# The causal mask of the prompt's attention: a product added to the logits, or GpSimd's affine_select on keep factors and betas

## The chip, the cores and the metric

The kernel runs on one core of one Trainium2 chip. The metric is device time in microseconds (us) of one execution. The kernel before took 1763.74 us, the median of 3 runs (1763.74 to 1766.75).

## What is computed

One layer of a hybrid decoder, for a prompt of 1024 new tokens and for 8 x 8 sampled tokens with a paged cache. An input projection feeds three mixers (RWKV-7, a short convolution, stick-breaking attention with 8 heads of 64); an output projection, a squared-ReLU MLP of 4096 and a gated per-layer embedding follow, all with residuals. The change lies in the prompt's stick-breaking attention:

```python
z = einsum('bqhd,bkhd->bhqk', q_blk, kf) * scale + bias_f
mask = k_pos[None, :] < q_pos[:, None]
log_beta = where(mask, log_sigmoid(z), -inf)
log_keep = where(mask, log_sigmoid(-z), 0.0)
later = cumsum(log_keep, axis=3, reverse=True) - log_keep
wts = exp(log_beta + later)
out = einsum('bhqk,bkhd->bqhd', wts, vf)
```

So a key at or after the query's own position has beta 0 and keep factor 1, and a weight is beta times the product of the keep factors of all later keys.

## The kernel before, in words

All products run on TensorE in fp32 split into a high and a low part (three matmuls for one). ScalarE makes the high part (a cast), VectorE or GpSimd the low part (a subtraction); for the MLP's weights that is the function `split_piece` (lines 1036 to 1044): the cast is L1042, the subtraction L1043 (GpSimd by default), and each piece has ten buffers. Weights come from memory through two raw buffers (L1036), with SyncE issuing the DMAs.

The attention is a generator, `attention`, called twice: for the query blocks of the first 512 positions (line 1006, interleaved with `convolution`, 5 of its emission steps to 4 of the attention's) and for the second 512 (line 1434). It goes over units (head, block of 256 queries), head outermost, and over two query tiles of 128 in each. For query tile i, `weights` handles the first L = 128 (i + 1) keys, in chunks of 512:

- L880: GpSimd writes a 1.0 behind the last keep factor.
- L884 and L887: two matmuls put q k into a PSUM bank (high and low parts stacked to 128 rows; q's parts are swapped in the second).
- L886: in the last chunk alone, between them, a third matmul adds `later` through the identity to the last 128 columns. `later` is 0 below the diagonal and -1e30 from it on; it is made once per call (lines 843 to 847) with a memset and an affine_select on GpSimd and a cast on ScalarE.
- L888 and L889: ScalarE takes the sigmoid of z + bias (beta) and of -z - bias (keep) from PSUM into SBUF.
- L890: VectorE turns keep into the running product from the right (a scan).
- L892: beta is multiplied by the shifted keep, on VectorE, or in the second call on GpSimd for odd tiles.

`values` runs AHEAD = 2 units later: it transposes the weights (L910, TensorE), splits them (L60 on ScalarE, L61 on VectorE) and multiplies them by v (L920, L921); L923 and L925 add the halves and a DMA stores the result. keep has 2 buffers in the first call and 3 in the second, beta 6 in both.

Around the attention, the first half runs beside the sampled tokens' RWKV part and the convolution (products L169 to L171), the second half beside the output projection, the MLP's `up` and the MLP's `down` of the first 512 positions (products L1062 to L1064). An `up` product of one bank has 24 matmuls, a `down` product 6. VectorE takes them out of three PSUM banks (`acc`): L1418 for `down`, L1351 for `up`, L1341 for the output projection. Between the two attention calls lie the load and transposes of the residual (L1248, L1249) and the first half of the output projection.

The program's order is not the order of the text: the framework (`schedule_with_timeline_sim=True`) writes each engine's queue by priority and by its own estimate of when each instruction is ready. Each engine then works through its queue strictly in that order, so that an instruction that waits holds all that stand behind it.

Of the kernel before, what the change touches and what calls it, by code (L numbers as in the profile page):

```python
# [21 lines left out]
F32 = mybir.dt.float32  # L22
F32R = mybir.dt.float32r
I32 = mybir.dt.int32
AF = mybir.ActivationFunctionType
ALU = mybir.AluOpType
# [22 lines left out]
def hybrid_step(ctx: ExitStack, tc: tile.TileContext, I, O):  # L49
    nc = tc.nc  # L50
    V, S, G, PE, SP = nc.vector, nc.scalar, nc.gpsimd, nc.tensor, nc.sync
# [4 lines left out]
    def f(t):  # L56
        return t.bitcast(F32)

    def split(dst_hi, dst_lo, src):
        S.copy(dst_hi, src)  # L60
        V.tensor_sub(dst_lo, src, f(dst_hi))  # L61
# [60 lines left out]
    ident_r = consts.tile([128, 128], F32R)  # L122
# [105 lines left out]
    for s in range(2):  # L228
        hs = slice(64 * s, 64 * s + 64)
        for q in range(2):  # L230
            for kind in range(2):
                m = mfull[hs, q, kind, :]
                G.affine_select(m, m, pattern=[[1, 64]], compare_op=ALU.is_ge, fill=0.0, base=-kind,
                                channel_multiplier=-1)
                if q:
                    m3 = m.rearrange("p (g r) -> p g r", r=NJ)
                    G.affine_select(m3, m3, pattern=[[-NJ, 8], [0, NJ]], compare_op=ALU.is_ge, fill=0.0, base=0,
                                    channel_multiplier=1)
                    G.affine_select(m3, m3, pattern=[[NJ, 8], [0, NJ]], compare_op=ALU.is_ge, fill=0.0,
                                    base=NJ - 1, channel_multiplier=-1)  # L240
# [523 lines left out]
    ap = tc.alloc_tile_pool(name="att_a", bufs=1, side="right", reuse_waits="tile")  # L764
# [73 lines left out]

    def attention(ap, q0, q1, zbank, wbank, obank, AHEAD):


        neg = ap.tile([128, 128], F32, name="neg_f")
        G.memset(neg, 0.0)
        G.affine_select(neg, neg, pattern=[[-1, 128]], compare_op=ALU.is_ge, fill=-1.0e30, base=-1,
                        channel_multiplier=1)
        later = ap.tile([128, 128], F32R, name="later")
        S.copy(later, neg)
        bias = ap.tile([128, 2, 8], F32, name="bias")
        src = I["sb_bias"]
        SP.dma_start(bias[:, 0], bass.AP(tensor=src.tensor, offset=src.offset, ap=[[0, 128], [1, 8]]))  # L850
        V.tensor_scalar(bias[:, 1], bias[:, 0], -1.0, None, op0=ALU.mult)

        heads = {}

        def prep(h):

            stk = []
            for name, n, r0 in (("k", 1, 0), ("q", 0, 256 * q0), ("x", 0, 256 * q0)):
                r = slice(r0, 256 * q1)
                o = ap.tile([128, 256 * q1 - r0], F32R, name=f"stk_{name}", bufs=2)  # L860
                if name == "x":
                    for e in range(2):
                        SP.dma_start(f(o)[64 * e:64 * e + 64], stk_s[n, h, 1 - e, :, r])
                else:
                    SP.dma_start(f(o), stk_s[n, h, :, :, r].rearrange("e d t -> (e d) t"))
                stk.append(o)
            vs = ap.tile([128, 2 * q1, 128], F32R, name="vs", bufs=2)
            SP.dma_start(f(vs), v_s[h, 0:2 * q1].rearrange("i p e -> p i e"))
            heads[h] = stk + [vs]

        wts = {}

        def weights(h, qb):
            kk, qa, qx, _ = heads[h]
            for i in (2 * qb, 2 * qb + 1):
                L = 128 * (i + 1)
                q = slice(i * 128 - 256 * q0, i * 128 + 128 - 256 * q0)
                beta = ap.tile([128, 256 * q1], F32, name="beta", bufs=2 * AHEAD + 2)
                keep = ap.tile([128, 256 * q1 + 1], F32, name="keep", bufs=3 if q0 else 2)
                G.memset(keep[:, L:L + 1], 1.0)  # L880
                for c0 in range(0, L, 512):
                    n = min(512, L - c0)
                    pz = zbank()
                    PE.matmul(pz[:, :n], qa[:, q], kk[:, c0:c0 + n], start=True, stop=False)  # L884
                    if c0 + n == L:
                        PE.matmul(pz[:, n - 128:n], ident_r, later, start=False, stop=False)  # L886
                    PE.matmul(pz[:, :n], qx[:, q], kk[:, c0:c0 + n], start=False, stop=True)  # L887
                    S.activation(beta[:, c0:c0 + n], pz[:, :n], AF.Sigmoid, bias=bias[:, 0, h:h + 1])  # L888
                    S.activation(keep[:, c0:c0 + n], pz[:, :n], AF.Sigmoid, bias=bias[:, 1, h:h + 1], scale=-1.0)  # L889
                V.tensor_tensor_scan(keep[:, 0:L][:, ::-1], keep[:, 0:L][:, ::-1], onesq[:, 0:1].to_broadcast([128, L]),  # L890
                                     1.0, op0=ALU.mult, op1=ALU.mult)
                (G if i % 2 and q0 else V).tensor_mul(beta[:, 0:L], beta[:, 0:L], keep[:, 1:L + 1])  # L892
                wts[h, i] = beta

        def values(h, qb):
            vs = heads[h][3]
            pr, s = divmod(h, 2)
            d = slice(64 * s, 64 * s + 64)
            po = obank()
            last_kt = 2 * qb + 1  # L900
            for g in range(qb + 1):
                pw = wbank()
                wh = ap.tile([128, 2, 256], F32R, name="wth", bufs=2)
                wl = ap.tile([128, 2, 256], F32R, name="wtl", bufs=2)
                p3 = pw.rearrange("p (k q) -> p k q", k=2)
                for e in range(2):
                    kt = 2 * g + e
                    for i in range(2):
                        if 2 * qb + i >= kt:
                            PE.transpose(p3[:, e, i * 128:i * 128 + 128],  # L910
                                         wts[h, 2 * qb + i][:, kt * 128:kt * 128 + 128], ident)
                if g < qb:
                    split(wh, wl, p3)
                else:
                    split(wh[:, 0], wl[:, 0], p3[:, 0])
                    split(wh[:, 1, 128:], wl[:, 1, 128:], p3[:, 1, 128:])
                for e in range(2):
                    kt = 2 * g + e
                    c = slice(128 if kt == last_kt else 0, 256)
                    PE.matmul(po[:, c], vs[:, kt, :], wh[:, e, c], start=kt == 0, stop=False)  # L920
                    PE.matmul(po[:, c], vs[:, kt, :], wl[:, e, c], start=False, stop=kt == last_kt)  # L921
            tmp = ap.tile([128, 256], F32, name="tmp", bufs=2)
            S.copy(tmp[0:64], po[64:128, 0:256])  # L923
            o32 = ap.tile([128, 256], F32, name="o32", bufs=2)
            V.tensor_add(o32[d], po[0:64, 0:256], tmp[0:64])  # L925
            SP.dma_start(mix_s[4 + pr, d, qb * 256:qb * 256 + 256], o32[d])

        units = [(h, qb) for h in range(8) for qb in range(q0, q1)]
        prep(0)
        for n in range(len(units) + AHEAD):  # L930
            if n < len(units):
                if n % (q1 - q0) == 0 and units[n][0] < 7:
                    prep(units[n][0] + 1)
                weights(*units[n])
            if n >= AHEAD:
                values(*units[n - AHEAD])
            yield
# [66 lines left out]

    wkv_sample_chunk(banks(2))
    conv, att = convolution(), attention(ap, 0, 2, banks(3, 4), banks(5, 6), banks(7), AA)
    run(*[conv] * CA[0], *[att] * CA[1])
    cv.release()
# [423 lines left out]
    first = [page(pre, "kpg", krows, 0, n, 4) for n in range(PAGES)]  # L1432
    ap = tc.alloc_tile_pool(name="att_b", bufs=1, side="right", reuse_waits="tile")
    run(attention(ap, 2, 4, banks(3, 4), banks(5, 6), banks(7), AB_))
    ap.release()
    dp = tc.alloc_tile_pool(name="dec", bufs=1, side="right", reuse_waits="tile")
# [118 lines left out]
```

## Time and profile before

| what | us |
|---|---|
| median of 3 runs | 1763.74 |
| lowest, highest | 1763.74, 1766.75 |
| the profiled execution | 1762.9 |
| its span in the trace | 1761.2 |

| engine | busy us | share | instructions |
|---|---|---|---|
| TensorE, matmuls (PE) | 1686.2 | 96% | 11741 |
| TensorE, weight loads (PEld) | 1502.5 | 85% | 11741 |
| VectorE (DVE) | 1108.7 | 63% | 1826 |
| ScalarE (ACT) | 774.7 | 44% | 1539 |
| GpSimd (POOL) | 662.8 | 38% | 636 |

Times within the span are us from its start. A matmul's duration runs into the next one's, because matmuls are pipelined: what one takes from the engine is seen in the distance of the starts. An instruction's line is that of the program; an idle time before an instruction is written in brackets, with what ended it. Some matmul records are missing in a trace.

### The profile page before, as it was taken

The page shows a single profiled execution, that of the slowest core. Times are in us where ns is not written, and L with a number is a line of the kernel's source. Part 1 is how long each engine was busy: PE and PEld are TensorE (multiplying, and loading weights), DVE is VectorE, ACT ScalarE, POOL GpSimd, SP SyncE. Part 2 cuts the span into 40 slices and gives each one's busy share as a digit, 9 for nine tenths or more (in the row PEclk, how much of TensorE's full clock was granted, in tenths as well). Part 3 has the DMA queues.
Part 4 walks back from the last instruction along what each step waited for, and adds up shares of the span by engine and source line. Part 5 has one row for each costly group of instructions (what it writes and reads, how often), then busy time and mean ns, then how long its engine had stood idle before and what let it go on. Part 6 is the DMA issues. An engine that isn't in the chain of part 4 may idle for free.

```text
span 1761.2 us, 30286 instructions
## 1 busy us (share of the span) xinstructions
PE 1686.2 (96%) x11741; PEld 1502.5 (85%) x11741; DVE 1108.7 (63%) x1826; ACT 774.7 (44%) x1539; POOL 662.8 (38%) x636
## 2 busy tenths in 40 slices
PE   6999899999999899999999999998899999999998
PEld 5898888888888777888876666897899999998898
DVE  6266963554576669888763344447978787777432
ACT  6633323333343667666542433445534444435421
POOL 4123321212310453422344552446855555535210
PEclk9999998999999899999999999999999999999999
DMA  5134456433622753433244443521332323222211
GB/s 183 50 114 133 110 148 170 117 97 110 159 74 83 234 178 113 128 117 107 89 137 138 147 149 112 182 73 49 108 97 87 94 84 94 88 84 72 75 51 39
DMA packets 206737, 196.98 MB, mean 112 GB/s; under 512 B 57793, under 2 KB 172129, under 8 KB 206466
## 3 DMA queue, kind: packets, MB, share of 16 engines
q1 hardware_dynamic: 201474, 178.27, 34.1%
q0 software_dynamic: 5120, 16.78, 3.2%
q8 instruction: 92, 1.51, 0.4%
q14 instruction: 51, 0.42, 0.1%
HBM read 158.02 MB, written 36.98 MB: 111 GB/s over the span
## 4 chain that ended last, share of the span: by engine, by line
PE 73%; DVE 11%; DMA 4%; issue 4%; ACT 3%; POOL 2%; SPq 2%; ACTq 0%; DVEq 0%; POOLq 0%
PE b L1062 12%; PE b L1064 12%; PE b L1063 12%; PE b L1382 3%; PE b L1381 3%; PE b L1380 3%; PE b L169 2%; PE b L170 2%; PE b L171 2%; PE b L790 2%; PE b L791 2%; PE b L792 1%; PE b L910 1%; DVE base_Q L281 1%; PE b L1172 1%
## 5 line engine op out<-in xcount | busy, mean ns | idle before, releaser
L1043 POOL TENSOR_TENSOR wl<-wr,wh 128x512 fp32r<-128x512 f32 x172 | 239.1, 1399 | 317.7 <-ACT wh L1042 309.3
L1042 ACT CAST wh<-wr 128x512 fp32r<-128x512 f32 x292 | 179.2, 623 | 328.0 <-PE b L1063 227.5
L1418 DVE TENSOR_TENSOR x<-b,x 128x288 f32<-128x288 f32 (+1 forms) x384 | 199.1, 528 | 107.8 <-PE b L1064 100.1
L1062 PE MATMUL b<-ah,wh 128*128 128x288 f32 (+1 forms) x768 | 257.3, 335 | 8.6 <-DVE x L1418 5.8
L1064 PE MATMUL b<-ah,wl 128*128 128x288 f32 (+1 forms) x768 | 253.8, 331 | 0.0
L1063 PE MATMUL b<-al,wh 128*128 128x288 f32 (+1 forms) x768 | 252.8, 329 | 0.0
L1062 PEld LDWEIGHTS b<-ah,wh 128*128 128x128 f32 x768 | 145.5, 190 | 24.3 <-DVE x L1418 8.8
L1062 PE MATMUL b<-nh,wh 128*128 128x512 f32 (+1 forms) x448 | 164.5, 368 | 0.9 <-DVE x L1418 0.9
L1063 PE MATMUL b<-nl,wh 128*128 128x512 f32 (+1 forms) x448 | 165.1, 369 | 0.0
L1064 PE MATMUL b<-nh,wl 128*128 128x512 f32 (+1 forms) x448 | 164.0, 366 | 0.0
L1064 PEld LDWEIGHTS b<-ah,wl 128*128 128x128 f32 x768 | 145.4, 189 | 14.4 <-issue 4.1
L1063 PEld LDWEIGHTS b<-al,wh 128*128 128x128 f32 x768 | 145.6, 190 | 8.9
L790 PE MATMUL b<-wh,h_hi 128*128 128x256 f32 x432 | 130.6, 302 | 3.1 <-ACT nat L797 3.1
L792 PE MATMUL b<-wh,h_lo 128*128 128x256 f32 x432 | 128.0, 296 | 0.0
L791 PE MATMUL b<-wl,h_hi 128*128 128x256 f32 x432 | 127.9, 296 | 0.0
L169 PE MATMUL b<-h_hi,wh 128*128 128x384 f32 (+1 forms) x336 | 115.2, 343 | 1.9 <-ACT xs L330 1.2
L890 DVE TENSOR_TENSOR_SCAN keep<-keep,onesq 128x128 f32<-128x128 f32 (+3 forms) x64 | 93.4, 1464 | 36.0 <-ACT keep L889 35.1
L170 PE MATMUL b<-h_lo,wh 128*128 128x384 f32 (+1 forms) x336 | 113.3, 337 | 0.3 <-DVE h_lo L201 0.3
L171 PE MATMUL b<-h_hi,wl 128*128 128x384 f32 (+1 forms) x336 | 112.2, 334 | 0.0
L1043 DVE TENSOR_TENSOR wl<-wr,wh 128x512 fp32r<-128x512 f32 x120 | 101.1, 845 | 7.6 <-PE b L1064 3.9
L159 POOL TENSOR_TENSOR wl<-wr,wh 128x1024 fp32r<-128x1024 f32 x26 | 68.8, 2653 | 93.9 <-ACT wh L158 93.9
L1043 POOL TENSOR_TENSOR wsl<-s,wsh 128x512 fp32r<-128x512 f32 x64 | 88.6, 1406 | 28.3 <-ACT wsh L1042 28.2
(417 smaller groups left out, 4340.0 us busy)
## 6 DMA issues: line engine op xcount, KB each, us to landing
wr<-in_w_up SPq DMA_DIRECT2D x64, 512.0 KB
wr<-in_w_down SPq DMA_DIRECT2D x64, 512.0 KB
wr<-in_w_in SPq DMA_DIRECT2D x26, 512.0 KB
wr<-in_w_out SPq DMA_DIRECT2D x16, 512.0 KB
xt<-in_x_prompt SPq DMA_DIRECT2D x8, 512.0 KB
stk_s<-sth SPq DMA_DIRECT2D x32, 128.0 KB
stk_s<-stl SPq DMA_DIRECT2D x32, 128.0 KB
out<-nat SPq DMA_DIRECT2D x16, 256.0 KB
```

The lines of the kernel that those rows point to most:

```text
L169: PE.matmul(ps[:, :n], wh[:, k, c], a, start=(k == 0), stop=False)
L170: PE.matmul(ps[:, :n], wh[:, k, c], b, start=False, stop=False)
L171: PE.matmul(ps[:, :n], wl[:, k, c], a, start=False, stop=(k == nk - 1))
L790: PE.matmul(o, a, w[0][:, k, :], start=(k == 0), stop=False)
L791: PE.matmul(o, a, w[1][:, k, :], start=False, stop=False)
L792: PE.matmul(o, b, w[0][:, k, :], start=False, stop=(k == 7))
L1042: S.copy(h3, src)
L1043: (sub or G).tensor_sub(l3, src, f(h3))
L1062: PE.matmul(ps[:, :n], w(0, k, m), a, start=(k == 0), stop=False)
L1063: PE.matmul(ps[:, :n], w(0, k, m), b, start=False, stop=False)
L1064: PE.matmul(ps[:, :n], w(1, k, m), a, start=False, stop=(k == nk - 1))
L1418: V.tensor_add(p.x[:, m, t0:t0 + n], ps[:, :n], p.x[:, m, t0:t0 + n])
```

## The change

The mask leaves the logits. `neg_f`, `later` and the product L886 are gone. After both sigmoids of all chunks of a query tile, GpSimd overwrites the last 128 columns of keep with 1.0 and those of beta with 0.0 wherever the key is not before the query, in place, with one affine_select each.

```diff
@@ -838,13 +838,6 @@
     def attention(ap, q0, q1, zbank, wbank, obank, AHEAD):
-        neg = ap.tile([128, 128], F32, name="neg_f")
-        G.memset(neg, 0.0)
-        G.affine_select(neg, neg, pattern=[[-1, 128]], compare_op=ALU.is_ge, fill=-1.0e30, base=-1,
-                        channel_multiplier=1)
-        later = ap.tile([128, 128], F32R, name="later")
-        S.copy(later, neg)
         bias = ap.tile([128, 2, 8], F32, name="bias")
@@ -882,11 +875,14 @@
                     PE.matmul(pz[:, :n], qa[:, q], kk[:, c0:c0 + n], start=True, stop=False)
-                    if c0 + n == L:
-                        PE.matmul(pz[:, n - 128:n], ident_r, later, start=False, stop=False)
                     PE.matmul(pz[:, :n], qx[:, q], kk[:, c0:c0 + n], start=False, stop=True)
                     S.activation(beta[:, c0:c0 + n], pz[:, :n], AF.Sigmoid, bias=bias[:, 0, h:h + 1])
                     S.activation(keep[:, c0:c0 + n], pz[:, :n], AF.Sigmoid, bias=bias[:, 1, h:h + 1], scale=-1.0)
+
+                for t, fill in ((keep, 1.0), (beta, 0.0)):
+                    own = t[:, L - 128:L]
+                    G.affine_select(own, own, pattern=[[-1, 128]], compare_op=ALU.is_ge, fill=fill, base=-1,
+                                    channel_multiplier=1)
                 V.tensor_tensor_scan(keep[:, 0:L][:, ::-1], keep[:, 0:L][:, ::-1], onesq[:, 0:1].to_broadcast([128, L]),
                                      1.0, op0=ALU.mult, op1=ALU.mult)
```

## Rows read from the trace of the kernel before

**Rows 1.** The page, engines: busy us (share of the span) xinstructions.

```profile
PE 1686.2 (96%) x11741; PEld 1502.5 (85%) x11741; DVE 1108.7 (63%) x1826; ACT 774.7 (44%) x1539; POOL 662.8 (38%) x636
```

**Rows 2.** Windows by stage: length, busy us of each engine, clock, DMA.

```profile
core 0: us, PE busy (x) PEld busy (x) DVE busy (x) ACT busy (x) POOL busy (x), PEclk, DMA share, GB/s
...
572.00:597.00 25.00, 18.02 (x126) 15.88 (x125) 21.17 (x34) 20.31 (x46) 8.03 (x12) 0.81 0.91 283
...
633.00:673.00 40.00, 37.93 (x175) 31.04 (x176) 33.45 (x35) 28.43 (x53) 21.70 (x18) 0.96 0.50 157
673.00:867.00 194.00, 192.59 (x1035) 163.98 (x1033) 162.97 (x206) 128.37 (x254) 60.57 (x62) 1.00 0.37 113
```

**Rows 3.** Waits of TensorE, 572 to 597: us in total, times, longest.

```profile
PE b L920 <- DVE o L925: 2.8, 1, 2.8
```

**Rows 4.** Waits, 633 to 867, of TensorE's start, VectorE and ScalarE.

```profile
PE b L910 <- POOL beta L892: 1.4, 1, 1.4
PE b L884 <- DMA stk_q<-stk_s: 1.4, 1, 1.4
...
DVE keep L890 <- ACT keep L889: 17.4, 18, 1.7
...
ACT wh L1042 <- PE b L1063: 22.2, 24, 2.5
```

**Rows 5.** The mask product L886: durations, and its count by stage.

```profile
L886 PE MATMUL b<-later,ident_r x64: 219/223/328, 469.8 to 859.1; 128*128 128x128 f32 x64
...
447.00:572.00 125.00, 5.75 (x24) 4.54 (x24) 0.99 0.38 104
572.00:597.00 25.00, 2.05 (x8) 1.80 (x8) 0.81 0.91 283
```

**Rows 6.** TensorE's timeline from 794.8: start, us, line, operands.

```profile
794.80 0.40 PE L884 MATMUL b<-stk_k,stk_q 128*128 128x512 f32 x1
...
795.27 0.39 PE L884 MATMUL b<-stk_k,stk_q 128*128 128x512 f32 x1
795.50 0.22 PE L886 MATMUL b<-later,ident_r 128*128 128x128 f32 x1
795.56 0.44 PE L887 MATMUL b<-stk_k,stk_x 128*128 128x512 f32 x1
795.84 0.39 PE L1062 MATMUL b<-ah,wh 128*128 128x512 f32 x1
```

**Rows 7.** Groups of GpSimd by shape: busy us, mean ns, idle before.

```profile
L237 POOL TENSOR_SCALAR_AFFINE_SELECT mfull<-mfull 64x64 f32<-64x64 f32 x4 | 2.0, 534 | 0.1
...
L844 POOL TENSOR_SCALAR_AFFINE_SELECT neg_f<-neg_f 128x128 f32<-128x128 f32 x2 | 0.6, 323 | 0.1
```

**Rows 8.** Timeline, a weight piece handed from ScalarE to GpSimd.

```profile
767.55 0.63 ACT L1042 CAST wh<-wr 128x512 fp32r<-128x512 f32 x1
...
768.26 1.29 POOL L1043 TENSOR_TENSOR wl<-wr,wh 128x512 fp32r<-128x512 f32 x1 [1.97 <-ACT wh L1042]
```

**Rows 9.** Groups, 652 to 867: GpSimd's multiply into beta.

```profile
L892 POOL TENSOR_TENSOR beta<-beta,keep 128x768 f32<-128x768 f32 (+1 forms) x16 | 31.4, 1962 | 55.4 <-DVE keep L890 52.1 <-PE b L887 3.4
```

**Rows 10.** Timeline of VectorE, and GpSimd's split beside it, 559 to 593.

```profile
559.18 0.41 DVE L892 TENSOR_TENSOR beta<-beta,keep 128x256 f32<-128x256 f32 x1
...
575.39 0.42 DVE L890 TENSOR_TENSOR_SCAN keep<-keep,onesq 128x128 f32<-128x128 f32 x1 [1.85 <-ACT keep L889]
...
576.94 1.27 POOL L1043 TENSOR_TENSOR wl<-wr,wh 128x512 fp32r<-128x512 f32 x1 [0.52 <-ACT wh L1042]
...
577.04 1.45 DVE L892 TENSOR_TENSOR beta<-beta,keep 128x256 f32<-128x256 f32 x1
...
592.58 1.23 DVE L890 TENSOR_TENSOR_SCAN keep<-keep,onesq 128x512 f32<-128x512 f32 x1 [0.41 <-ACT keep L889]
```

**Rows 11.** Groups of VectorE by shape, 633 to 870: two scans.

```profile
L890 DVE TENSOR_TENSOR_SCAN keep<-keep,onesq 128x896 f32<-128x896 f32 x8 | 16.9, 2118 | 4.7 <-ACT keep L889 4.7
...
L890 DVE TENSOR_TENSOR_SCAN keep<-keep,onesq 128x640 f32<-128x640 f32 x8 | 11.9, 1490 | 5.9 <-ACT keep L889 5.4 <-POOL keep L880 0.5
```

## The prediction, made before the change was run

> **What bounds the kernel now.** I read the page first: TensorE is busy for 1686.2 of 1761.2 us [rows 1]. Then the windows by stage around the attention [rows 2]: the prompt's first half with the convolution as cover (447 to 572), a tail of eight query tiles after the convolution (572 to 597), and, past 633, the second half under the MLP's matmuls, with a ragged start and a dense rest. The reader is to see that TensorE stands for 25.00 - 18.02 = 7.0 us in the tail, while from 673 to 867 it is busy for 192.59 of 194.00 us, VectorE for 162.97 and GpSimd for only 60.57. So TensorE sets the pace, except in the tail; there the longest of its waits is one for VectorE's last addition of the attention, 2.8 us [rows 3]. At the second half's ragged start it waits twice, 1.4 us each, for the DMA of a query stack and for GpSimd's multiply into beta [rows 4].
>
> **What is removed.** 64 mask products, one per query tile: 24 before 572, 8 in the tail, 32 in the second half [rows 5]. Their durations (223 ns) overlap with those of their neighbours and are no price; I take starts instead [rows 6]. Two products of 512 columns without a mask take 795.27 - 794.80 = 0.47 us, the same two with the mask between them 795.84 - 795.27 = 0.57 us: 0.10 each there. In the tiles of 384, 256 and 128 columns the same subtraction gives 0.10 to 0.12. I take 0.11; bounds 0.06 (from the mask's start to the next product's, 795.50 to 795.56) and the 0.223 of its duration. Where TensorE is the bound all of it comes off: 24 + 32 = 56 products, 56 x 0.11 = **-6.2 us**. The eight of the tail I count at nothing, since TensorE waits there anyway. The two setups of the mask (memset, affine_select, cast) also go. I count them at nothing: at the second half's start, where the first product could wait for the mask, it waits for the DMA of its query stack [rows 4]; if the DMA came earlier, the 0.3 us of one affine_select could show. No DMA is added, removed or moved.
>
> **What is added.** Two affine_selects of 128x128 per query tile, 128 in all, on GpSimd. The same form took 323 ns on average; a 64x64 one with another pattern took 534, which is the upper bound [rows 7]. 128 x 0.32 = 41 us on an engine that is idle for 194 - 60.6 = 133 us of the dense stretch alone: as work it is free. What counts is where it stands. The scan (L890) followed ScalarE's keep sigmoid directly; now the keep affine_select stands between. Handing over to GpSimd costs 0.08 us (a cast ends at 767.55 + 0.63 = 768.18, the split begins at 768.26 [rows 8]), so each scan is ready 0.32 + 0.08 = **0.40 us later**. Bounds: nothing (the new order puts other VectorE work in front of the scan), and 0.53 + 0.08 + 1.96, when a multiply of GpSimd stands in front [rows 9]. I take 0.40, since GpSimd is mostly idle. The beta select follows 0.32 us later, under a scan of 0.42 us or more, and is hidden by it. If it weren't, the multiply, which in the second half runs on GpSimd itself for odd tiles, would be late by that 0.32.
>
> Where do 0.40 us count? In the dense stretch, nowhere: the weights of a tile are transposed two units (four tiles) after they are asked for, and VectorE already waits for the keep sigmoid 18 times, up to 1.7 us, without TensorE noticing [rows 4]. Behind a waiting affine_select on GpSimd stand the splits of the MLP's weights (L1043). They have ten buffers, and ScalarE, which feeds them, itself waits 24 times for TensorE to free one [rows 4]: a split may be late by microseconds. What would be late next, if that cover went, is the weight load of the next product.
>
> In the tail the cover is gone. Two of its eight scans find VectorE idle for the keep sigmoid (575.39 and 592.58), and the others share VectorE with work that is ready [rows 10]. I charge four tiles, between none and all eight: 4 x 0.40 = **+1.6 us**. At the start of the second half the 1.4 us wait for the multiply grows by one tile's 0.40: **+0.4 us** (bounds 0 and three tiles, 1.2).
>
> Sum: -6.2 + 1.6 + 0.4 = **-4.2 us**. The profiled execution took 1762.9 us (span 1761.2 and 1.7 around it), 0.84 less than the median of the runs, 1763.74. I take the difference off the median: **1759.5 us**. With the masks at 0.10 to 0.12 and the delays from none to 4.4 (eleven tiles), this case alone spans 1757.0 to 1762.5.
>
> **Sharing with VectorE.** A row speaks against the change: VectorE's multiply of 128x256 took 0.41 us at 559.18 and 1.45 at 577.04, when GpSimd ran a split from 576.94 [rows 10]. Two engines that read the same memory slow each other here, and in the tail VectorE has only 25.00 - 21.17 = 3.8 us to spare [rows 2]. No row shows whether a one-input affine_select does the same, so it is a rival, below.
>
> The Trainium skill, page "GPSIMD Engine Reference", section "1. Specifications", says that GpSimd's SBUF interfaces are shared with VectorE and contend with VectorE instructions that have two SBUF inputs. The scan and the multiply are such instructions; the trace agrees for the split (0.41 against 1.45 us). By that rule the sum would be +0.2 in place of -4.2.
>
> **The rivals.**
> (a) *VectorE slows beside each affine_select.* Each 0.32 us is added to VectorE. In the second half 64 x 0.32 = 20.5 us fit into its idle 40.00 - 33.45 + 194.00 - 162.97 = 37.6 us. In the tail 16 x 0.32 = 5.1 stand in place of 1.6, at the start of the second half 4 x 0.32 = 1.3 in place of 0.4: +4.4, so 1763.9. For it: the row just named (the page's rule is this case). Against: an affine_select reads one tensor, and few will overlap. Chance 0.09.
> (b) *The first half falls behind.* With two keep buffers its 24 covered tiles may each slip 0.40 us, 9.6 us in all, some two tiles at (572 - 470) / 24 = 4.25 us each, and these then stand without cover at 7.0 / 8 = 0.9 us: +1.8. All eight tail tiles are late as well, +1.6: 1762.9. Against it: the tiles come in bursts with pauses, so slips are made up. Chance 0.10.
> (c) *Slower: the scan queues behind GpSimd's multiply.* In the second half, a tile after an odd one may have its keep affine_select behind the odd tile's multiply (1.96 us, 16 times [rows 9]). Then the scan starts 1.96 + 0.40 = 2.4 us late and VectorE stands, with TensorE's PSUM evictions behind it. TensorE has three banks (`acc`); a down product fills one with 6 matmuls of 512 columns, 6 x 0.23 = 1.4 us (0.47 / 2 each), so VectorE may be away for 2.8 us. It decides when wait and scan together exceed that: 2.4 + 1.49 - 2.8 = 1.1 us eight times, 2.4 + 2.12 - 2.8 = 1.7 eight times [rows 11], 22 us; half of it, as the up products (24 matmuls to a bank) hide it: +11, 1770.5. For it: VectorE has little idle time. Against: GpSimd has 133 us free, and scans of 2 us pass without a stall today. Chance 0.18.
> (d) *The whole order is drawn anew.* The framework orders each engine's queue from its own estimate of the times, so 64 instructions less and 128 more can shift waits anywhere; before the attention and in the decoding, TensorE waits too. No part of the change sets the sign: 1754 to 1769. Chance 0.16, half of it faster, a third slower.
>
> **How the numbers follow.** The forecast has the remaining 0.47; its own span reaches over the bound of 0.2% (3.5 us, about what a measurement of this kernel can tell from no change, at 1760.2 and 1767.3), so 0.36 of it is faster and 0.11 the same. Faster: 0.36 + 0.08 = 0.44. Same: 0.11 + 0.09 + 0.10 + 0.03 = 0.33. Slower: 0.18 + 0.05 = 0.23. The range runs from just below (d)'s lower end to just past (c): 1753 to 1772.
>
> **What would show it.** Right: L884 and L887 follow each other within 0.47 us; the dense stretch is shorter by 32 x 0.11 = 3.5 us; affine_selects of 0.3 us with idle GpSimd time before them; the tail's TensorE idle time grows from 7.0 to about 8.6. Wrong: TensorE waits for evictions (L1418, L1351) in the second half, with scans waiting for GpSimd (c); multiplies that are stretched beside affine_selects (a); a tail of ten tiles (b); a shift in a stretch where no attention runs (d).

## The result, and the profile after

The changed kernel took 1752.03 us, the median of 5 runs (1744.33 to 1755.4), beside 1765.42 us of the kernel before in runs of the same kind (1763.74 to 1770.02). The ratio is 0.991, with a 95% interval of 0.9885 to 0.9935: faster by 0.9%. The two medians lie 13.4 us apart (0.8%), three times the 4.2 us forecast, and the time is 1 us below the range's lower end. The profiled execution took 1755.4 us, the longest of its five, so a comparison of the two traces shows less than the medians do: spans of 1753.7 and 1761.2 us, 7.5 us apart.

In the code after, L877 and L878 are the two products of a logit bank, L879 and L880 the sigmoids, L884 the affine_selects, L886 the scan, L888 the multiply, L906 the transposes, L916 and L917 the products with v, L921 the last addition, L1376 what is L1380 before. The page, engines, of the kernel after:

```profile
PE 1678.3 (96%) x11677; PEld 1494.9 (85%) x11677; DVE 1118.4 (64%) x1826; ACT 774.1 (44%) x1537; POOL 714.3 (41%) x760
```

Against [rows 1] TensorE has 64 instructions less and GpSimd 124 more (128 selects, less two memsets and two selects of the setups) and 51.5 us more of work. The sizes in time aren't to be read here. Windows put them in place. They are cut at six milestones that both traces have: the attention's first product, the convolution's last product (L171), the first product of the output projection, the first product of the attention's second half, its last product with v, and the last transpose of keys in the decode (the sampled tokens' attention). The first two bound what is called the first stage below, the second and third the tail. Before:

```profile
core 0: us, PE busy (x) PEld busy (x) DVE busy (x) ACT busy (x) POOL busy (x), PEclk, DMA share, GB/s
469.70:572.60 102.90, 99.52 (x796) 87.83 (x796) 69.01 (x126) 46.98 (x106) 8.00 (x28) 0.98 0.29 83
572.60:595.40 22.80, 15.82 (x118) 13.97 (x117) 19.57 (x31) 18.71 (x43) 6.71 (x12) 0.83 0.90 282
595.40:633.50 38.10, 36.17 (x170) 29.17 (x168) 15.49 (x31) 16.71 (x35) 24.21 (x25) 0.97 0.62 178
633.50:902.30 268.80, 265.48 (x1396) 225.15 (x1397) 216.06 (x274) 170.34 (x332) 91.31 (x84) 0.99 0.37 115
902.30:1067.30 165.00, 160.72 (x798) 112.70 (x797) 68.13 (x111) 60.80 (x114) 83.53 (x91) 0.98 0.52 156
```

The same five stages after:

```profile
469.05:564.50 95.45, 95.00 (x772) 83.83 (x772) 67.12 (x126) 47.28 (x106) 27.56 (x76) 1.00 0.30 85
564.50:589.10 24.60, 17.43 (x124) 14.57 (x123) 19.65 (x37) 20.86 (x49) 14.38 (x28) 0.82 0.91 301
589.10:620.70 31.60, 30.03 (x135) 24.32 (x134) 13.96 (x23) 12.05 (x25) 21.81 (x21) 0.93 0.69 193
620.70:899.10 278.40, 272.06 (x1396) 228.83 (x1397) 227.12 (x279) 172.82 (x338) 117.28 (x151) 0.99 0.38 111
899.10:1056.80 157.70, 154.92 (x789) 108.64 (x788) 68.58 (x110) 59.23 (x111) 83.17 (x90) 1.00 0.54 163
```

The convolution's stage is 7.45 us shorter, with 24 TensorE instructions less, and TensorE stands in it for 0.45 us (95.45 - 95.00) where it stood for 3.4; the clock there rises from 0.98 to 1.00. The second half is longer by 9.6 us and the stages on either side of it shorter by 6.5 and 7.3: 1396 instructions in both, of which 32 were mask products before, so MLP products have moved in from the neighbours. Stage by stage the last three can't be compared; from the output projection's first product to the first product of `up` for the second 512 positions (L1380, the same work in every kernel) it is 623.7 us before and 621.2 after.

**Where the first stage's time came from.** The timeline at its start, before (start, us, engine, line, operands, and in brackets the idle time and its end):

```profile
469.71 0.22 PE L884 MATMUL b<-stk_k,stk_q 128*128 128x128 f32 x1
469.77 0.27 PE L886 MATMUL b<-later,ident_r 128*128 128x128 f32 x1
471.63 0.32 PE L708 MATMUL b<-ident,s_in 64*64 64x64 f32 x2 [1.58 <-DMA s_in<-in_state_wkv]
471.88 0.33 PE L887 MATMUL b<-stk_k,stk_x 128*128 128x128 f32 x1
...
472.22 0.22 PE L886 MATMUL b<-later,ident_r 128*128 128x128 f32 x1
472.37 1.14 PE L708 MATMUL b<-ident,s_in 64*64 64x64 f32 x30
473.44 0.39 PE L887 MATMUL b<-stk_k,stk_x 128*128 128x256 f32 x1
...
477.11 1.15 PE L708 MATMUL b<-ident,s_in 64*64 64x64 f32 x32
...
479.08 0.69 ACT L888 ACTIVATE beta<-b,bias 128x512 f32<-128x512 f32 x1 [0.18 <-PE b L887]
...
482.14 2.36 POOL L159 TENSOR_TENSOR wl<-wr,wh 128x1024 fp32r<-128x1024 f32 x1 [3.87 <-ACT wh L158]
482.48 2.78 DVE L892 TENSOR_TENSOR beta<-beta,keep 128x512 f32<-128x512 f32 x2
...
485.11 0.74 PE L910 MATMUL b<-ident,beta 128*128 128x128 f32 x3 [1.80 <-DVE beta L892]
```

And after:

```profile
469.05 0.22 PE L877 MATMUL b<-stk_k,stk_q 128*128 128x128 f32 x1
469.11 0.27 PE L878 MATMUL b<-stk_k,stk_x 128*128 128x128 f32 x1
469.83 0.32 PE L708 MATMUL b<-ident,s_in 64*64 64x64 f32 x2 [0.45 <-DMA s_in<-in_state_wkv]
...
475.34 0.69 ACT L879 ACTIVATE beta<-b,bias 128x512 f32<-128x512 f32 x1 [1.02 <-PE b L878]
...
475.64 1.15 PE L708 MATMUL b<-ident,s_in 64*64 64x64 f32 x32
...
478.26 0.69 DVE L888 TENSOR_TENSOR beta<-beta,keep 128x512 f32<-128x512 f32 x1
...
479.24 2.55 POOL L159 TENSOR_TENSOR wl<-wr,wh 128x1024 fp32r<-128x1024 f32 x1
```

L708 transposes the sampled tokens' state, which comes by DMA. Before, it stood in TensorE's queue inside the groups of the first two tiles (a group is the products of one logit bank, from the first to the last), between the mask product and L887: the first group waited 1.58 us in its middle, the second ran 1.1 us of transposes before its last product. After, both groups are whole and L708 stands behind each. The fourth tile's group moved most: before, it stood behind a third run of L708 (477.11) and began 8.5 us into the stage (478.19); after, it stands ahead of that run (475.64) and began at 5.6 (474.68). Its beta sigmoid (512 columns) started 9.4 us after the stage's first product before (479.08), 6.3 after (475.34). So its multiply came at 482.48, beside GpSimd's split of a weight piece, and two of them took 2.78 us; after, it came at 478.26, ahead of that split, and took 0.69. TensorE's wait for it, 1.80 us, is gone, and with it a stretch at half the clock: windows of the granted clock (the column behind POOL), before

```profile
485.00:489.00 4.00, 3.90 (x15) 3.70 (x16) 4.00 (x6) 1.69 (x4) 2.56 (x3) 0.57 0.00 0
```

and after

```profile
485.00:489.00 4.00, 4.00 (x27) 3.87 (x26) 3.68 (x7) 2.38 (x5) 2.94 (x7) 1.00 0.56 174
```

TensorE is as busy in the one as in the other, but starts 15 instructions there in place of 27. Three terms make up most of the stage's 7.45 us: the 24 products less, 24 x 0.11 = 2.6; TensorE's waits, 3.38 - 0.45 = 2.9; and the slow stretch, where eight distances of 384-column products, 485.98 to 488.69, take 2.7 us and 8 x 0.17 = 1.4 would do, so 1.3. Together that is 6.8, an estimate.

### The profile page after: what moved, and what is told of

It is laid out like the page before. It is cut to its first block, busy times and chain, and to the rows that moved or that the text cites. A ratio compares the mean times of both kernels' runs of the same rounds, so it can differ in the third digit from the quotient of the medians.

```text
span 1753.7 us, 30271 instructions
## 1 busy us (share of the span) xinstructions
PE 1678.3 (96%) x11677; PEld 1494.9 (85%) x11677; DVE 1118.4 (64%) x1826; ACT 774.1 (44%) x1537; POOL 714.3 (41%) x760
## 4 chain that ended last, share of the span: by engine, by line
PE 73%; DVE 12%; DMA 5%; issue 5%; ACT 2%; POOL 2%; SPq 1%; ACTq 0%; POOLq 0%; DVEq 0%
PE b L1058 13%; PE b L1059 12%; PE b L1060 12%; PE b L1378 3%; PE b L1377 3%; PE b L1376 3%; PE b L169 2%; PE b L170 2%; PE b L171 2%; PE b L790 2%; PE b L791 2%; PE b L906 2%; PE b L792 1%; DVE base_Q L281 1%; DMA wr<-in_w_out 1%
## 5 line engine op out<-in xcount | busy, mean ns | idle before, releaser
L1039 POOL TENSOR_TENSOR wl<-wr,wh 128x512 fp32r<-128x512 f32 x172 | 247.0, 1445 | 298.7 <-ACT wh L1038 258.6
L1414 DVE TENSOR_TENSOR x<-b,x 128x288 f32<-128x288 f32 (+1 forms) x384 | 198.9, 527 | 103.0 <-PE b L1060 101.5
L171 PE MATMUL b<-h_hi,wl 128*128 128x384 f32 (+1 forms) x336 | 112.2, 334 | 0.0
L886 DVE TENSOR_TENSOR_SCAN keep<-keep,onesq 128x128 f32<-128x128 f32 (+3 forms) x64 | 94.7, 1481 | 24.5 <-POOL keep L884 24.3
```

The costliest lines, as they stand in the source:

```text
L171: PE.matmul(ps[:, :n], wl[:, k, c], a, start=False, stop=(k == nk - 1))
L1039: (sub or G).tensor_sub(l3, src, f(h3))
L1414: V.tensor_add(p.x[:, m, t0:t0 + n], ps[:, :n], p.x[:, m, t0:t0 + n])
```

## Experiments

All were timed in five rounds beside the kernel before, in three groups. Theory, at the start (A in the expectations): the removed products, where TensorE sets the pace, are the gain. Rival (B): the queues' new order is. C, put after the first four runs, names the part of the order: the place of the first groups in TensorE's queue.

**after_again.** The changed kernel a second time, no edit.

> The changed kernel once more, beside the others. If the measured gain (13 us by the medians, 7.5 between the two profiled executions) is a property of the program, its median lies 11 to 15 us under the kernel before here too. If the difference between 7.5 and 13 is scatter from execution to execution, the two medians lie 7 to 15 us apart, and the spread of either is several us.

1751.78 us (6 runs), ratio 0.992 (0.9892 to 0.9949). The gain repeats. Its stages are those of the first trace within 0.2 us up to the output projection (95.3 and 24.5); from there to L1380 it took 618.7, so 2.5 us of that long stretch is one execution's difference from another.

**no_mask.** Neither products nor selects; the causal mask is left out.

```diff
-                    if c0 + n == L:
-                        PE.matmul(pz[:, n - 128:n], ident_r, later, start=False, stop=False)
...
```

The set-up of the mask goes too.

> The mask is left out altogether (the output is that of an attention without the causal mask): no product, no affine_select. Theory A, prices: 64 products x 0.11 us = 7 us come off, and nothing waits for GpSimd, so it is 7 us faster than before and 0 to 2 us faster than the changed kernel would be by prices alone. Theory B, the order: what was gained beyond 6 us comes from the newly drawn order of the queues, so this third order may land anywhere from 2 to 20 us under the kernel before, and the waits in the convolution's stage differ from both.

1753.37 us (7 runs), ratio 0.9936 (0.9911 to 0.9961): no faster than the kernel that has 128 selects more. The first stage is 95.5 us, as after; the tail, with no select in it, is 25.6, the longest of all kernels.

**both_masks.** The products stay, and the selects come in.

```diff
                     S.activation(keep[:, c0:c0 + n], pz[:, :n], AF.Sigmoid, bias=bias[:, 1, h:h + 1], scale=-1.0)
+                for t, fill in ((keep, 1.0), (beta, 0.0)):
+                    own = t[:, L - 128:L]
+                    G.affine_select(own, own, pattern=[[-1, 128]], compare_op=ALU.is_ge, fill=fill, base=-1,
+                                    channel_multiplier=1)
```

> The product stays and the two affine_selects per tile are added. Theory A, prices: the affine_selects cost 2 us (four tail tiles and one start tile at 0.40), so 0 to 4 us slower than before. Theory B, the order: another draw, 5 us or more from the kernel before in either direction; faster than before by 3 us or more would show that the gain does not come from the removed product.

1755.34 us (12 runs), ratio 0.9952 (0.9933 to 0.9971). Work was only added, and the kernel is 8 to 9 us faster than before. Its first stage is 103.0 us, with the first two groups cut; its tail is 21.0 and its decode 156.5 in place of 165.0. No sum of the prices above can come out so.

**mask_last.** The same 64 products, each third in its group in place of second.

```diff
-                    if c0 + n == L:
-                        PE.matmul(pz[:, n - 128:n], ident_r, later, start=False, stop=False)
-                    PE.matmul(pz[:, :n], qx[:, q], kk[:, c0:c0 + n], start=False, stop=True)
+                    PE.matmul(pz[:, :n], qx[:, q], kk[:, c0:c0 + n], start=False, stop=c0 + n < L)
+                    if c0 + n == L:
+                        PE.matmul(pz[:, n - 128:n], ident_r, later, start=False, stop=True)
```

> The same work as before, with the mask product as the third of its group in place of the second. Theory A, prices: no difference, within 1.5 us. Theory B, the order: the framework draws a new order, and the time moves by 3 us or more either way though no work has changed.

1765.55 us (12 runs), ratio 0.9997 (0.9977 to 1.0017): no change. L708 stands again inside the first group (it waited 1.79 us there), now ahead of the mask product, and the first stage is 102.7 us. Theory A had no difference here, and so it came. If B holds, not every edit of this place redraws the order to advantage.

**head0_only and all_but_head0.** The change for 4 of the 64 tiles (head 0 of the first half), and for the other 60.

```diff
-                    if c0 + n == L:
+                    if c0 + n == L and not (not q0 and h == 0):
...
+                for t, fill in ((keep, 1.0), (beta, 0.0)) if not q0 and h == 0 else ():
```

all_but_head0 has the two conditions the other way round; the set-up of the mask stays in both.

> The change for 4 of 64 tiles alone: head 0 of the first half (its 4 tiles get affine_selects, all others keep the product). Theory A, prices: 4 x 0.11 = 0.4 us, within 1 us of before. Theory C, the place: in the queue of TensorE the first group of products (L884, L886, L887) is cut by a transpose of the sampled tokens' state (L708) that waits for a DMA; without the third product the group is whole and in front of it. Then the stage from the attention's first product to the convolution's last falls from 102.9 us to 97.5 to 99, the 2.0 us wait for the multiply at 482.9 and the half-clock stretch behind it are gone, and the kernel is 3 to 6 us faster.

> The change for 60 of 64 tiles: all but head 0 of the first half. Theory A, prices: 60/64 of the gain, so 10 to 12 us faster than before, the convolution's stage at about 96 us. Theory C, the place: that stage keeps the cut group, the 2.0 us wait and the half-clock stretch, and is only 20 x 0.11 = 2.2 us shorter, 100.5 to 101.5; the kernel is 5 to 9 us faster, with what the second half gives.

Four tiles: 1751.09 us (6 runs), ratio 0.9917 (0.9887 to 0.9948). Sixty tiles: 1764.18 (12 runs), 0.9989 (0.9965 to 1.0013). Four tiles bring the whole gain, the other sixty, with 60 products less, nothing that can be measured. Both theories missed these times: C had the four at 3 to 6 us faster, where 14 came, and the sixty at 5 to 9, where 1 came; A had 0.4 and 10 to 12. C's first stage came for the four tiles (97.5 to 99 expected) and for the sixty within 0.2 us. First stages: 98.1 and 101.7 us; the 20 other products of that stage are worth 1.2 to 2.6 us (102.9 - 101.7; 98.1 - 95.5), near 20 x 0.11 = 2.2, the place of the first groups 4.8.

**first_half and second_half.** The change in one call of the attention alone.

```diff
-                    if c0 + n == L:
+                    if c0 + n == L and q0:
...
+                for t, fill in ((keep, 1.0), (beta, 0.0)) if q0 == 0 else ():
```

second_half has the two conditions the other way round.

> The change in the first half's call alone. Theory C: the convolution's stage at 95.3 to 95.6 us as in the changed kernel, 7.4 us gained there; from the output projection's first product on as before (623 to 626 us), with the wait of over 4 us for a page of keys in the decoding and the half-clock stretch behind it. In all 6 to 9 us faster. Theory A, prices: 32 x 0.11 less what the tail costs: 1 to 3 us faster.

> The change in the second half's call alone. Theory C: the convolution's stage stays at 102.7 to 103.0; the second half gains its 32 x 0.11 = 3.5 us and the decoding's wait for a page of keys falls to 2.4 us or less with no half-clock stretch behind it, another 2 to 5 us: 4 to 8 us faster. Theory A, prices: 3 to 4 us faster, and the wait for the page as before, over 4 us.

1762.25 us (0.9983, 0.9965 to 1.0002) and 1767.33 us (1.0021, 0.9999 to 1.0043), 12 runs each. In first_half the groups are whole and the first stage is 96.1 us, but from the output projection to L1380 it takes 630.0: the 6 us are given back. In second_half the 32 products that the forecast priced at 3.5 us are gone, and that stretch takes 624.6, 0.9 more than before, and the wait for a page of keys is still 4.1. Neither time can be told from that of the kernel before, and C, which had them at 6 to 9 and 4 to 8 us faster, missed both. A came near with 1 to 3 us for first_half and missed second_half (3 to 4). The parts don't add up to the whole (-3 and +2 against -13), so the prices of the parts weren't the cause.

**What the decode shows.** The sampled tokens' attention takes its cached keys page by page, each by a DMA. TensorE's transposes of a page of keys, and what ended its idle time before them (us, times); kernel before:

```profile
L1167 PE MATMUL b<-ident,kpg x128: 270/273/473, 902.5 to 1067.4; 128*128 128x128 f32 x128
its engine sat idle before it (us, times) until:
  DMA kpg<-in_cache_k,idx: 4.1, 1
```

It is 4.1 to 4.4 us in before, mask_last, no_mask, all_but_head0, first_half and second_half, but 2.7 after (2.0 in after_again), 1.8 in both_masks and 0.5 in head0_only. It costs more than itself: timeline of before behind it,

```profile
926.62 1.11 PE L1167 MATMUL b<-ident,kpg 128*128 128x128 f32 x4 [4.12 <-DMA kpg<-in_cache_k,idx]
927.39 0.77 PE L1062 MATMUL b<-ah,wh 128*128 128x512 f32 x1
...
931.80 0.63 PE L1063 MATMUL b<-al,wh 128*128 128x512 f32 x1
932.23 0.52 PE L1064 MATMUL b<-ah,wl 128*128 128x512 f32 x1
...
935.14 0.40 PE L1063 MATMUL b<-al,wh 128*128 128x512 f32 x1
935.37 0.39 PE L1064 MATMUL b<-ah,wl 128*128 128x512 f32 x1
```

Products of 512 columns start 0.43 us apart at 932 and 0.23 at 935. From 927.39 to 932.23 there are 11 distances, 4.84 us where 11 x 0.23 = 2.5 would do: 2.3 us on top of the 4.1.

So the theory is now that the place of 4 tiles' products in TensorE's queue is the whole cause. The direct trial keeps all work and changes the place alone.

**whole_group and all_but_head0_whole.** The framework is asked to put the second and third product of head 0's groups in the first half straight behind the first; in the kernel before, and in all_but_head0.

```diff
                     PE.matmul(pz[:, :n], qa[:, q], kk[:, c0:c0 + n], start=True, stop=False)
-                    if c0 + n == L:
-                        PE.matmul(pz[:, n - 128:n], ident_r, later, start=False, stop=False)
-                    PE.matmul(pz[:, :n], qx[:, q], kk[:, c0:c0 + n], start=False, stop=True)
+                    with (tc.high_priority() if not q0 and h == 0 else ExitStack()):
+                        if c0 + n == L:
+                            PE.matmul(pz[:, n - 128:n], ident_r, later, start=False, stop=False)
+                        PE.matmul(pz[:, :n], qx[:, q], kk[:, c0:c0 + n], start=False, stop=True)
```

> All 64 mask products stay and no affine_select is added; the only edit asks the framework to place the second and third product of head 0's tiles in the first half (16 products' neighbours at most) straight behind the first one, so that no transpose of L708 stands inside a group. Theory 'place': in the queue of TensorE this kernel has head 0's groups where the changed kernel has them, and from there to the decode the order that the kernel with 4 changed tiles has. The stage from the first product of the attention's first half to the last of the convolution takes 97.5 to 99 us (102.9 before, 98.1 with the 4 tiles changed), the stretch at half clock inside it is gone, TensorE's wait for a page of keys in the decode is under 1.5 us (4.2 to 4.5 before), and the time is 1750 to 1753 us, though nothing of the mask's work has gone. Theory 'work' (rival: the removed products and the affine_selects' own times make the gain): the time is that of the kernel before, within 2 us, 1763 to 1767.

> 60 of the 64 tiles changed, head 0 of the first half keeps its 4 mask products, and the products of these 4 groups are placed one behind the other. Without the placing this kernel took 1764.2 us. Theory 'place': its queue is now that of the changed kernel with 4 products added, so it takes 1751 to 1755 us, the convolution stage 95.5 to 97. Theory 'work': placing 4 groups is worth at most the 4 products' 0.5 us, 1763 to 1765.

whole_group: 1753.64 us (8 runs), ratio 0.9927 (0.99 to 0.9955). No instruction of the mask has gone or come, and the gain is there, 0.7% beside 0.9% with intervals that overlap; the time is 0.6 us above the range that theory "place" gave. all_but_head0_whole: 1749.40 us (6 runs), 0.9911 (0.988 to 0.9941), 15 us faster than all_but_head0, which has the same instructions, and 1.6 us below its expected range. Theory "place" holds, "work" falls. whole_group's page, engines, has the instructions of [rows 1], one for one:

```profile
PE 1683.0 (96%) x11741; PEld 1501.6 (86%) x11741; DVE 1104.1 (63%) x1826; ACT 776.6 (44%) x1539; POOL 668.9 (38%) x636
```

Its timeline at the attention's start (L884, L887 and L888 are the three products):

```profile
469.96 0.22 PE L884 MATMUL b<-stk_k,stk_q 128*128 128x128 f32 x1
470.02 0.27 PE L887 MATMUL b<-later,ident_r 128*128 128x128 f32 x1
470.13 0.27 PE L888 MATMUL b<-stk_k,stk_x 128*128 128x128 f32 x1
471.04 0.33 PE L708 MATMUL b<-ident,s_in 64*64 64x64 f32 x2 [0.64 <-DMA s_in<-in_state_wkv]
```

its clock in the window where the kernel before had the half-clock stretch (0.96 there, as in mask_last),

```profile
480.00:520.00 40.00, 40.00 (x329) 37.50 (x330) 27.14 (x53) 18.52 (x47) 5.73 (x12) 1.00 0.17 55
```

and its wait for pages of keys:

```profile
L1168 PE MATMUL b<-ident,kpg x128: 270/273/331, 891.7 to 1050.2; 128*128 128x128 f32 x128
its engine sat idle before it (us, times) until:
  DMA kpg<-in_cache_k,idx: 0.2, 1
```

The first stage takes 98.5 us, as with the 4 tiles changed (98.1). No line of the edit touches the decode, 420 us later, yet the wait there falls from 4.1 to 0.2 us: the products of the MLP stand in other places between the pages. Counted in the traces, the products with weights between the decode's first five runs of page transposes are 19, 11, 27 and 12 before, and the same in mask_last; they are 20, 17, 23 and 16 in whole_group, and the same in head0_only. In all_but_head0_whole the first stage took 97.5 us where 95.5 to 97 were expected; its longest wait of TensorE there is another one, 1.3 us for a keep sigmoid.

**twice.** The changed kernel with every select issued a second time.

```diff
-                for t, fill in ((keep, 1.0), (beta, 0.0)):
+                for t, fill in ((keep, 1.0), (beta, 0.0), (keep, 1.0), (beta, 0.0)):
```

> The changed kernel with both affine_selects issued a second time on every tile (the result is the same): 128 more of 0.29 us on GpSimd. Theory 'added work is dear': each of the 64 tiles' scans starts some 0.6 us later, and where TensorE waits for it (4 tiles of the tail, the start of the second half) that is 2.4 to 3.0 us, 1754 to 1756. Theory 'the order decides': the longer path is hidden but for the tail's 2.4, and what the queue's new order does to the decode's pages is worth more than that either way: its order around the pages is that of the kernel with 4 changed tiles, so the wait for a page is under 1.5 us and the time 1750 to 1755.

1753.75 us (10 runs), ratio 0.9939 (0.9917 to 0.9962). By time the two theories can't be told apart. By stage they can: the tail, where a longer path of each tile should have shown, is 23.2 us, shorter than with single selects (24.6), and no transpose of keys waits for a page's DMA.

**pages5_after.** The changed kernel with a fifth buffer for pages of keys.

```diff
-                    kpg = first.pop(0) if first else page(pre, "kpg", krows, b, n, 4)
+                    kpg = first.pop(0) if first else page(pre, "kpg", krows, b, n, 5)
```

> The changed kernel with five buffers for pages of keys in the decode instead of four (it fits since the two tiles of the mask are gone). If TensorE's wait for a page in the decode (2.3 us there, 1.4 in the second profile) comes from a buffer that is late, it is gone and the time is 1749 to 1751; if it comes from the page's gather itself, issued when the decode's first pages are, a fifth page is on its way earlier and the queue's order is drawn anew: the time is within 3 us of 1752 on either side, and the wait stands at the sixth page instead of the fifth.

1750.61 us (7 runs), ratio 0.9917 (0.9884 to 0.9951). The wait for pages is gone altogether, and the time lies in both of the ranges expected; the interval lies over that of the change itself: a microsecond or two can't be told here. That the buffer alone did it isn't shown, since the order is another one too.

The kernels side by side, in us; "cut" says whether L708 stands inside a product group of the first two tiles, the first stage runs to the convolution's last product, the tail to the output projection's first:

| kernel | groups | first stage | tail | output projection to L1380 | wait for pages | median |
|---|---|---|---|---|---|---|
| before | cut | 102.9 | 22.8 | 623.7 | 4.1 | 1763.7 to 1765.4 |
| mask_last | cut | 102.7 | 22.7 | 625.5 | 4.4 | 1765.6 |
| all_but_head0 | cut | 101.7 | 25.1 | 622.2 | 4.4 | 1764.2 |
| second_half | cut | 102.4 | 23.0 | 624.6 | 4.1 | 1767.3 |
| both_masks | cut | 103.0 | 21.0 | 620.7 | 1.8 | 1755.3 |
| first_half | whole | 96.1 | 23.8 | 630.0 | 4.3 | 1762.3 |
| no_mask | whole | 95.5 | 25.6 | 617.1 | 4.3 | 1753.4 |
| after | whole | 95.5 | 24.6 | 621.2 | 2.7 | 1752.0 |
| twice | whole | 93.3 | 23.2 | 623.7 | 0 | 1753.8 |
| head0_only | whole | 98.1 | 23.1 | 617.3 | 0.5 | 1751.1 |
| whole_group | whole | 98.5 | 20.8 | 617.7 | 0.2 | 1753.6 |
| all_but_head0_whole | whole | 97.5 | 23.0 | 615.2 | 1.9 | 1749.4 |
| pages5_after | whole | 95.1 | 24.4 | 616.9 | 0 | 1750.6 |

The four kernels with cut groups and a long wait take 1764 to 1767 us, the six with whole groups and a wait of at most 2.7 take 1749 to 1754, the three that have one of the two lie at 1753 to 1762. Several are level with the change and none is measurably faster.

What "cut" stands for is more than the wait for the DMA. In all five kernels with cut groups the fourth tile's group stands behind the third run of L708 and begins 7.3 to 8.7 us into the first stage, and TensorE waits 1.8 to 2.3 us for VectorE about 15 us into it. In the eight with whole groups it begins at 5.1 to 6.2 us, and no such wait is longer than 0.43 us. The wait for the DMA inside the first group does not set the length of the first stage: it was 0.46 us in all_but_head0 and 0.65 in both_masks, with stages of 101.7 and 103.0, and 1.58 in before with 102.9. The cut and the fourth group's place were not tried apart.

## Why the prediction was wrong

The likeliest outcome, a gain, came, but from another cause than the one priced: that the direction fits is luck.

- **The sum's frame** failed: "Where TensorE is the bound all of it comes off: 24 + 32 = 56 products". It holds the order of every queue fixed. The price itself stands (after, two pairs of 512-column products start at 762.60 and 763.06, 0.46 us apart, against 0.57 with a mask), and in the first stage the 20 products of the other heads are worth 1.2 to 2.6 us. But the second half's 32 alone gave no gain, and the whole gain is had with 4 products less, or with none less.
- **Rival (d)** named the mechanism, and its reason was the step that failed: "No part of the change sets the sign". In the first stage a part did: with head 0's groups whole, L708 stands behind them, and the stage is 4.8 us shorter in head0_only. The trace of before has L708 at 471.63, waiting for a DMA between the mask product and L887. The forecast weighs waits from 572 on alone and takes the first half as covered. With the first half's rows a price was at hand: the 1.80 us wait at 485 and the half-clock stretch behind it. For what lies behind that stage no row of before gives a sign: both_masks was 9 us faster with its groups cut, first_half only 3 with them whole. What (d) named as its sign, a shift where no attention runs, came in the decode (165.0 to 157.7 us). Its 1754 to 1769 ended 2 us above what came.
- **The select's 0.40 us** was a little short, 0.54 in this row: the median select took 0.295 us (0.285 to 1.7), and the third tile's scan began 0.57 us after its sigmoid ended (473.75 + 0.57 = 474.32 to 474.89), against 0.03 us before (475.83 + 0.58 = 476.41 to 476.44). The framework put beta's select ahead of keep's, which the forecast had the other way round. Over all tiles VectorE waited 24.3 us for keep's select, 21 times, against 35.1 us, 30 times, for the sigmoid before.
- **The tail, +1.6**, came out as +1.8 and is no confirmation: without any select it is 25.6 us, with two pairs 23.2. Its length goes with the order, and TensorE stood in it for 7.2 us (24.60 - 17.43) against 7.0, not the 8.6 expected.
- **The second half's start, +0.4**, and the **dense stretch, -3.5**, can't be read: products moved across both. Together with the decode they gave -2.5 (621.2 - 623.7) in one execution and -5.0 in the other.
- **(a)** did not happen as priced. The rows of the kernel after:

```profile
472.06 0.42 DVE L886 TENSOR_TENSOR_SCAN keep<-keep,onesq 128x128 f32<-128x128 f32 x1 [6.99 <-POOL keep L884]
472.10 0.48 POOL L884 TENSOR_SCALAR_AFFINE_SELECT beta<-beta 128x128 f32<-128x128 f32 x1
472.52 0.29 DVE L888 TENSOR_TENSOR beta<-beta,keep 128x128 f32<-128x128 f32 x1
472.53 0.43 POOL L884 TENSOR_SCALAR_AFFINE_SELECT keep<-keep 128x128 f32<-128x128 f32 x1
...
524.04 0.29 POOL L884 TENSOR_SCALAR_AFFINE_SELECT beta<-beta 128x128 f32<-128x128 f32 x1
524.12 0.49 DVE L886 TENSOR_TENSOR_SCAN keep<-keep,onesq 128x128 f32<-128x128 f32 x1 [0.45 <-POOL keep L884]
```

In the first four rows the scan and the multiply, which began first, last as long as in the kernel before (0.42 and 0.29), and the selects beside them took 0.48 and 0.43 in place of 0.29. In the last two the select began first and kept its 0.29 us, and the scan took 0.49 in place of 0.42. So the one that started second paid; for VectorE's scans and multiplies beside selects that was never more than 0.09 us, where (a) charged 0.32 for each of 128. VectorE's busy time did grow, by 9.7 us (1108.7 to 1118.4); 4.1 of it lies on the eight scans of 1024 columns (3.14 us on average against 2.63), and none of these ran beside a select. The Trainium skill, page "GPSIMD Engine Reference", section "1. Specifications", says that GpSimd's SBUF interfaces contend with VectorE instructions that have two SBUF inputs. The trace agrees as to who meets whom: the scan and the multiply have two such inputs, and a select that began inside an addition with one input in PSUM kept its 0.29 us (733.80, inside L1414 from 733.65 to 734.33).

- **(b)** fell: the first stage got shorter, and the tail holds eight tiles' last products in both kernels. **(c)** fell: scans of the second half did wait for a select, 5 times, up to 3.1 us, but TensorE's one wait for an eviction there is 0.9 us, as long as the one in the kernel before. The kernel after, waits from 625 to 859 (engine, line, waited for: us, times, longest):

```profile
DVE keep L886 <- POOL keep L884: 9.5, 5, 3.1
...
PE b L1058 <- DVE x L1337: 0.9, 1, 0.9
```

**What stays open.** No run shows why the framework puts L708 inside the group when three products are there, and behind it when two are. How much of the stretch behind the output projection is the wait for pages, and how much the rest of the order, wasn't tried by itself; first_half, at 630.0 us, has the wait of the kernel before and is 6 us longer still. Executions of one kernel lie up to 18 us apart (the kernel before, 1756.98 to 1775.02, in the second group), so differences of 2 us between single traces carry nothing.

## What to carry to other kernels

Where a framework draws the queues, the price of an edit can be the smaller part of what it does: try it with the order held, or move the same instructions with no work removed, before the removed work is credited. Look in the queue of the bounding engine for work that stands in the middle of a group on which others wait; here one line of priority that moved it behind was worth 11 us (1764.3 to 1753.6). And list the longest waits of the bounding engine in the whole span, not only near the edit: in whole_group one of 4.1 us fell to 0.2 over 400 us behind the edited lines.

## What the runs showed of the hardware

Two waits of TensorE cost more than their length: behind the 1.80 us at 485 it ran at a granted clock of 0.57 on average over 4 us, and behind the 4.1 us at 926 its 512-column products were 0.43 us apart, the lower of its two clock levels (1.2 GHz, 2.4 at 0.23 us), for at least 4.8 us. Not every wait did: behind the 1.58 us at 471 products of 320 columns start 0.15 us apart (473.66, 473.81, 473.96), as they do at 570 (569.70, 569.85, 570.00).

In the rows where GpSimd and VectorE meet, the one that started second took longer: the select 0.48 in place of 0.29 us, begun 0.04 us into a scan; the scan 0.49 in place of 0.42, begun 0.08 us into a select. A larger price is VectorE's at 479.85 in the kernel after: a multiply of 128 columns began when a split on GpSimd had 1.94 us still to go (479.24 + 2.55 = 481.79), and took 2.09 us where it takes 0.29.
